# A 64-byte gap in on-chip memory ahead of the weight tiles of a streaming encoder

## The chip, the core and the metric

One core of a Trainium2 chip runs the kernel. The metric is the device time of one execution in microseconds (us). Five engines work side by side: TensorE (PE in the profile, with its weight loads listed apart as PEld), VectorE (DVE), ScalarE (ACT), GpSimd (POOL) and SyncE (SP, which only issues DMAs). All operands of the engines lie in SBUF, 128 partitions side by side, and a tile is a byte range that is the same in every partition.

## The reference

Two layers over 512 tokens of width 1024, in float32:

```
for l in (0, 1):
    h = rmsnorm(x, norm_mix_g[l])
    if l == 0:  mix = mlstm(conv+silu(h @ a_w_in)) * sigmoid(o)     # 4 heads of 192
    else:       mix = band_attention(h @ b_w_in, K, V, rel_bias)    # 12 heads of 64
    x = x + concat(mix, memory_attention(h, mem @ mem_w_kv[l])) @ w_out
    u, g = split(rmsnorm(x, norm_ffn_g[l]) @ ffn_w_up[l])           # 2 x 2816 columns
    x = x + (silu(causal_dwconv(g)) * u) @ ffn_w_down[l]
    if l == 0:  K, V = split(rmsnorm(x, kv_norm_g) @ w_kv)
return rmsnorm(x, final_g)
```

## The kernel before

Activations are kept transposed: a tile of 128 features by 512 tokens, `KT = 8` such tiles for the width. Each float32 operand of a product is split in two rounded halves, `hi` and `lo`, and each product is three matmuls, `hi*hi + lo*hi + hi*lo`. The rounding to `hi` is a copy on ScalarE (line 130), and `lo` is a subtraction on VectorE (line 131). The three matmuls are lines 169, 170 and 171:

```
def split(hi, lo, src, on_act=True, pinned=False):
    high = A.copy(hi, src) if on_act else V.tensor_copy(hi, src)
    low = V.tensor_tensor(out=lo, in0=src, in1=f(hi), op=ALU.subtract)
...
def mm3(o, lh, ll, rh, rl, first, last, more=False):
    nc.tensor.matmul(o, lh, rh, start=first, stop=False, skip_group_check=more)
    nc.tensor.matmul(o, lh, rl, start=False, stop=False, skip_group_check=more)
    nc.tensor.matmul(o, ll, rh, start=False, stop=last, skip_group_check=more)
```

A weight block of 128 by 1024 comes by a DMA of SP's queue into a raw tile `wr` (`load`, line 143) and is split by `parts` into `wh` and `wl`. In `project` and its relatives the blocks of `wh` and `wl` are the stationary operand, 128 columns at a time, and the activations (`u` tiles) stream past, 512 or 256 columns each. In `value_columns`, in the value products of the memory and in the last projection it is the other way round: `u` is stationary and `wh`, `wl` stream.

All tiles of one tag come from one pool with a fixed count of buffers:

```
bufs = {"wr": 3, "wh": 3, "wl": 3, "u": 57, "t": 8, "pt": 2, "s": 16, "rb": 3, "bias": 4}
```

`u` holds activations and their halves, `t` scratch, `pt` probabilities (and, in the channel mixer, raw gate weights), `s` small columns of 32 numbers (sums, reciprocals), `rb` the row of the norm, broadcast over the partitions, `bias` the exponents and relative biases that POOL's queue brings (lines 1029, 1325, 1407). Constants lie in a pool of their own ahead of these: `ident`, `ones`, `onesr` (a 128x128 tile of ones, the stationary operand where a sum over partitions is spread, lines 244 and 274), the columns of norm gains.

The pool lays its tags out in the order in which the program first asks for them, each with its count of buffers, so where a tile lies follows from the text. The built program has these offsets, in bytes in each partition (before the change):

| tag | bytes of one | first one at | modulo 512 |
|---|---|---|---|
| `ident`, `ones`, `onesr` | 512 | 16512, 17024, 17536 | 128 |
| `u` | 2048 | 20544 | 64 |
| `pt` | 10240 | 137280 | 64 |
| `wr` | 4096 | 157760 | 64 |
| `t` | 2048 | 170048 | 64 |
| `s` | 128 | 186432 | 64 |
| `wh` | 4096 | 188480 | 64 |
| `wl` | 4096 | 200768 | 64 |
| `rb` | 2048 | 213056 | 64 |
| `bias` | 2048 | 219200 | 64 |

The order of the work on PE, ACT and DVE is written out by hand in most of the kernel: generators for the attention heads are woven with generators for projections, and the channel mixer's steps are listed one by one. SP's loads run ahead as far as the three `wr` buffers let them.

Of the kernel before, what the change touches and what calls it, by code (L numbers as in the profile page):

```python
# [9 lines left out]
F32 = mybir.dt.float32  # L10
# [6 lines left out]
P = 128  # L17
# [38 lines left out]
def trunk(  # L56
# [22 lines left out]
    pool = ctx.enter_context(tc.tile_pool(name="pool", bufs=1))  # L79
    psum = ctx.enter_context(tc.tile_pool(name="psum", bufs=1, space=bass.MemoryType.PSUM))  # L80

    bufs = {"wr": 3, "wh": 3, "wl": 3, "u": 57, "t": 8, "pt": 2, "s": 16, "rb": 3, "bias": 4}
# [4 lines left out]
    def sb(tag, shape, dtype=F32):  # L87
        count[0] += 1
        return pool.tile(shape, dtype, tag=tag, name=f"{tag}{count[0]}", bufs=bufs[tag])
# [5 lines left out]
    def small(n=4):  # L95
        return sb("s", [P, 32])[:, :n]
# [278 lines left out]

    memT, xT = [], []
    norm = Norm()
    ss = small(2 * TT).rearrange("p (c t) -> p c t", c=2)

    def square(T, c, on_act):  # L380
# [1142 lines left out]
```

## Time and profile before

| | us |
|---|---|
| median of 3 runs | 1195.89 |
| lowest, highest | 1195.11, 1197.09 |
| the profiled execution: time | 1195.72 |
| its span, first to last instruction | 1194.0 |
| PE busy | 1183.5 (99%) |
| DVE busy | 961.7 (81%) |
| ACT busy | 725.2 (61%) |
| POOL busy | 130.3 (11%) |
| mean granted TensorE clock | 0.999 |

The profiled execution spends 1195.72 - 1194.0 = 1.72 us outside its span. A matmul is listed with the time from its start to the modelled end of its pipeline, so neighbours overlap, and PE's pace is read from the distance between starts. Under a line number stand all instructions that this line issued; names are the program's tiles without their buffer numbers, output first.

### The profile page before, as it was taken

The numbers are of one execution on the slowest core, as the hardware profiler recorded it, in microseconds if no ns is written. First come the engines' busy times: TensorE is split into PE (matmuls) and PEld (weight loads), VectorE is DVE, ScalarE is ACT, GpSimd is POOL, SyncE is SP. The second block draws the span as 40 slices with busy tenths as digits, with TensorE's granted clock in tenths as the row PEclk, the third lists the DMA queues.
The fourth block names the chain that finished last, engine by engine and source line by source line (L and its number), as shares of the span: only waits on it lengthen the run. The fifth ranks groups of instructions, "written<-read, shape, count | busy, mean of one in ns | idle before, by whom it ended". The sixth has DMA issues, their size and how long they took to land.

```text
span 1194.0 us, 18184 instructions
## 1 busy us (share of the span) xinstructions
PE 1183.5 (99%) x6719; PEld 1037.0 (87%) x6719; DVE 961.7 (81%) x1760; ACT 725.2 (61%) x1294; POOL 130.3 (11%) x222
## 2 busy tenths in 40 slices
PE   9999999999999999999999999999999999999997
PEld 9988888888899998999888888888889988999986
DVE  6877788788978888888698888997896888888855
ACT  5648677655656555555576677776565655555545
POOL 1211201010021111111020000101001011011100
PEclk9999999999999999999999999999999999999999
DMA  8645313444265676665464313246336455665551
GB/s 289 212 108 140 84 54 80 152 144 141 88 156 147 156 165 165 154 144 123 142 204 123 89 54 101 69 135 185 111 99 141 116 139 135 142 141 139 119 158 71
DMA packets 200155, 158.61 MB, mean 133 GB/s; under 512 B 8344, under 2 KB 179838, under 8 KB 200066
## 3 DMA queue, kind: packets, MB, share of 16 engines
q1 hardware_dynamic: 183906, 119.74, 34.1%
q0 software_dynamic: 15584, 36.67, 14.9%
q8 instruction: 53, 0.87, 0.3%
q10 hardware_dynamic: 576, 1.05, 0.2%
q14 instruction: 36, 0.29, 0.1%
HBM read 128.89 MB, written 32.46 MB: 135 GB/s over the span
## 4 chain that ended last, share of the span: by engine, by line
PE 92%; ACT 3%; DVE 2%; DMA 1%; SPq 1%; issue 0%; POOL 0%; POOLq 0%; DVEq 0%; ACTq 0%
PE pmm L169 15%; PE pmm L170 15%; PE pmm L171 15%; PE ptr L171 6%; PE ptr L169 6%; PE ptr L170 6%; PE pmm L785 6%; PE psc L171 5%; PE psc L170 5%; PE psc L169 5%; PE pmm L784 3%; PE psc L519 2%; PE ptr L1350 1%; DMA wr<-in_mem_w_kv_dram 1%; PE ptr L1371 1%; PE ptr L1372 1%
## 5 line engine op out<-in xcount | busy, mean ns | idle before, releaser
L169 PE MATMUL pmm<-u,wh 128*128 128x512 f32 (+1 forms) x872 | 309.1, 355 | 0.3 <-ACT u L130 0.2
L170 PE MATMUL pmm<-u,wh 128*128 128x512 f32 (+1 forms) x872 | 306.2, 351 | 0.0
L171 PE MATMUL pmm<-u,wl 128*128 128x512 f32 (+1 forms) x872 | 306.0, 351 | 0.0
L131 DVE TENSOR_TENSOR wl<-wr,wh 128x1024 fp32r<-128x1024 f32 (+3 forms) x172 | 199.8, 1163 | 57.0 <-ACT wh L130 55.0
L130 ACT CAST wh<-wr 128x1024 fp32r<-128x1024 f32 (+3 forms) x172 | 172.4, 1004 | 97.7 <-PE pmm L170 44.5
L171 PEld LDWEIGHTS pmm<-u,wl 128*128 128x128 f32 x872 | 164.5, 189 | 21.1
L169 PEld LDWEIGHTS pmm<-u,wh 128*128 128x128 f32 x872 | 164.5, 189 | 18.5 <-ACT u L130 1.1
L170 PEld LDWEIGHTS pmm<-u,wh 128*128 128x128 f32 x872 | 164.7, 189 | 18.2 <-DVE u L131 0.5
L169 PE MATMUL ptr<-u,wh 128*128 128x512 f32 x272 | 106.7, 392 | 0.0
L171 PE MATMUL ptr<-u,wl 128*128 128x512 f32 x272 | 106.1, 390 | 0.0
L753 POOL DMA_DIRECT2D xspill<-t x64 | 55.6, 869 | 461.1 <-ACT t L752 450.4
L170 PE MATMUL ptr<-u,wh 128*128 128x512 f32 x272 | 105.9, 389 | 0.0
L130 ACT CAST u<-pt 128x512 fp32r<-128x512 f32 x102 | 63.0, 620 | 46.8 <-DVE pt L875 46.7
L131 DVE TENSOR_TENSOR u<-pt,u 128x512 fp32r<-128x512 f32 x102 | 69.9, 688 | 11.2 <-ACT u L130 8.5
L169 PE MATMUL psc<-u,wh 128*128 128x256 f32 (+1 forms) x232 | 76.1, 328 | 0.0
L171 PE MATMUL psc<-u,wl 128*128 128x256 f32 (+1 forms) x232 | 75.9, 327 | 0.0
L170 PE MATMUL psc<-u,wh 128*128 128x256 f32 (+1 forms) x232 | 75.9, 327 | 0.0
L937 ACT ACTIVATE t<-t 128x512 f32<-128x512 f32 x34 | 21.6, 634 | 79.3 <-DVE t L660 79.3
L785 PE MATMUL pmm<-u,u 128*128 128x512 f32 x192 | 69.6, 397 | 0.0
L821 DVE TENSOR_TENSOR t<-t,pmm 128x256 f32<-128x256 f32 x72 | 30.2, 419 | 44.9 <-ACT t L819 44.8
L752 ACT COPY t<-ptr 128x512 f32<-128x512 f32 x64 | 37.4, 585 | 43.1 <-PE ptr L171 43.1
L660 DVE SCALAR_TENSOR_TENSOR t<-t,cols,t 128x511 f32<-128x511 f32 x80 | 59.7, 746 | 3.7 <-ACT t L667 3.7
(300 smaller groups left out, 2673.8 us busy)
## 6 DMA issues: line engine op xcount, KB each, us to landing
wr<-in_ffn_w_up_dram SPq DMA_DIRECT2D x54, 512.0 KB, 4.2
wr<-in_ffn_w_down_dram SPq DMA_DIRECT2D x38, 512.0 KB, 4.1
pt<-in_ffn_w_up_dram SPq DMA_DIRECT2D x34, 512.0 KB, 6.2
xspill<-t POOLq DMA_DIRECT2D x64, 256.0 KB, 5.2
wr<-in_a_w_in_dram SPq DMA_DIRECT2D x20, 512.0 KB, 3.7
xspill<-u POOLq DMA_DIRECT2D x32, 256.0 KB, 2.6
u<-xspill SPq DMA_DIRECT2D x32, 256.0 KB, 5.0
wr<-in_w_kv_dram SPq DMA_DIRECT2D x12, 512.0 KB, 3.7
```

Of the source, the lines that this page charges most:

```text
L130: high = A.copy(hi, src) if on_act else V.tensor_copy(hi, src)
L131: low = V.tensor_tensor(out=lo, in0=src, in1=f(hi), op=ALU.subtract)
L169: nc.tensor.matmul(o, lh, rh, start=first, stop=False, skip_group_check=more)
L170: nc.tensor.matmul(o, lh, rl, start=False, stop=False, skip_group_check=more)
L171: nc.tensor.matmul(o, ll, rh, start=False, stop=last, skip_group_check=more)
L519: nc.tensor.matmul(o, a, b, start=first and i == 0, stop=i == 1)
L660: V.scalar_tensor_tensor(acc[:, n:], src[:, : S - n], self.fw[:, c * FT + j : c * FT + j + 1], acc[:, n:], op0=ALU.mult, op1=ALU.add,)
L752: A.copy(t, o)
L753: G.dma_start(xspill[j], t, accum_op=ALU.add)
L784: nc.tensor.matmul(r[:, :H], w[1][:, k], p[i - 1][:, :H], start=False, stop=False, skip_group_check=True)
L785: nc.tensor.matmul(r, w[0][:, k], p[i - 1], start=False, stop=k == n - 1, skip_group_check=True)
L821: V.tensor_tensor(out=o, in0=o, in1=r[:, H:], op=ALU.add)
```

## The change

A tile of 16 numbers (64 bytes in each partition) is requested from the pool with a tag of its own, after `u`, `pt`, `wr` and `t` have been asked for, and ahead of the first `s`. Nothing writes or reads it.

```diff
     memT, xT = [], []
     norm = Norm()
+    pool.tile([P, 16], F32, tag="gap", name="gap", bufs=1)
     ss = small(2 * TT).rearrange("p (c t) -> p c t", c=2)
```

In the built program `s`, `wh`, `wl`, `rb` and `bias` start 64 bytes later than before (at 128 modulo 512); `u`, `pt`, `wr`, `t` and all constants lie where they lay. Every engine has the same instructions, in the same order and with the same waits; of the operands only these offsets differ. The line numbers after line 377 are higher by one.

## The prediction

> **What bounds the kernel now.** I read the page's busy shares first, then the chain of work that ended last, then what PE waited for.
>
> ```profile
> PE 1183.5 (99%) x6719; PEld 1037.0 (87%) x6719; DVE 961.7 (81%) x1760; ACT 725.2 (61%) x1294; POOL 130.3 (11%) x222
> PE 92%; ACT 3%; DVE 2%; DMA 1%; SPq 1%; issue 0%; POOL 0%; POOLq 0%; DVEq 0%; ACTq 0%
> 300.00:590.00 290.00, 290.00 (x1811) 262.16 (x1810) 239.02 (x381) 166.53 (x287) 42.13 (x56) 1.00 0.58 141
> 860.00:1160.00 300.00, 300.00 (x1855) 270.44 (x1854) 244.83 (x388) 170.63 (x293) 27.35 (x32) 1.00 0.54 132
> 1160.00:1194.00 34.00, 26.92 (x149) 22.44 (x148) 16.41 (x44) 17.01 (x37) 0.00 (x0) 0.95 0.16 62
> ```
>
> PE is busy for 1183.5 of 1194.0 us and carries 92% of the chain. The last three lines are from the busy time by stage (columns: length, then PE, PEld, DVE, ACT, POOL with counts, the granted clock, the DMA share, GB/s): in the two channel mixers PE has no gap at all, while DVE works 239.0 of 290 us and ACT 166.5. Of PE's 10.5 us of idle time 34.00 - 26.92 = 7.1 lie in the last 34 us. So the time is PE's pace, matmul after matmul. As no engine gets another instruction or another wait, only one question is left: does any instruction or transfer take another time when some of its operands lie 64 bytes further on?
>
> **How many instructions meet a moved tile.** The groups of weight loads give the count for `wh` and `wl`.
>
> ```profile
> L169 PEld LDWEIGHTS pmm<-u,wh 128*128 128x128 f32 x872 | 164.5, 189 | 18.5 <-ACT u L130 1.1
> L169 PEld LDWEIGHTS ptr<-u,wh 128*128 128x128 f32 x272 | 51.2, 188 | 8.5
> L169 PEld LDWEIGHTS psc<-u,wh 128*128 128x128 f32 x232 | 44.0, 190 | 4.5
> L784 PEld LDWEIGHTS pmm<-u,wl 128*128 128x128 f32 x96 | 18.3, 191 | 0.0
> L785 PEld LDWEIGHTS pmm<-u,wh 128*128 128x128 f32 x96 | 18.1, 189 | 3.4
> ```
>
> Lines 170 and 171 have as many as line 169, so 3 x (872 + 272 + 232) + 96 + 96 = 4320 of 6719 matmuls take their stationary operand from a moved tile. That makes the resolution of the question plain: 0.2% of the time, 2.4 us, about what a measurement of this kernel can tell from no change, is 2.4 / 4320 = 0.56 ns for each of these loads.
>
> **PE's pace before.** Two steady trains, in order of start (start us, duration us); the lines between go on in the same step.
>
> ```profile
> 601.16 0.39 PE L169 MATMUL pmm<-u,wh 128*128 128x512 f32 x1
> ...
> 605.92 0.39 PE L169 MATMUL pmm<-u,wh 128*128 128x512 f32 x1
> ...
> 394.28 0.28 PE L170 MATMUL pmm<-u,wh 128*128 128x256 f32 x1
> ...
> 395.48 0.28 PE L171 MATMUL pmm<-u,wl 128*128 128x256 f32 x1
> ```
>
> From 601.16 to 605.92 there are 21 starts, 4.76 / 21 = 0.2267 us each, for 512 columns; from 394.28 to 395.48 there are 10, 0.120 us each, for 256. The difference, 107 ns, is the price of 256 columns, so each matmul carries 120 - 107 = 13 ns that are not columns. In the first train ACT and DVE split the next block into `wh` and `wl` and DMAs fill `wr` at the same time, and the step stays the same: nothing that runs beside it is seen in it.
>
> **Stationary operands, 4320 loads.** The trace has no load from `wh` at the new place, but it has loads from a tile that lies as `wh` will: the constant `onesr`, at 128 modulo 512, with the streaming tiles at 64 modulo 512, which is just the relation after the change.
>
> ```profile
> L244 PEld LDWEIGHTS psc<-t,onesr x10: 186/188/192, 30.0 to 248.6; 128*128 128x128 f32 x10
> L274 PEld LDWEIGHTS psc<-t,onesr x6: 186/188/188, 280.2 to 841.6; 128*128 128x128 f32 x6
> 600.03 0.39 PE L170 MATMUL pmm<-u,wh 128*128 128x512 f32 x1
> 600.03 0.19 PEld L171 LDWEIGHTS pmm<-u,wl 128*128 128x128 f32 x1
> 280.21 0.39 PE L171 MATMUL pmm<-u,wl 128*128 128x512 f32 x1
> 280.43 0.63 PE L274 MATMUL psc<-t,onesr 128*128 128x512 f32 x2
> 626.09 0.39 PE L171 MATMUL pmm<-u,wl 128*128 128x512 f32 x1
> 626.32 0.65 PE L274 MATMUL psc<-t,onesr 128*128 128x512 f32 x2
> 248.11 0.39 PE L169 MATMUL ptr<-u,wh 128*128 128x512 f32 x1
> 248.33 0.40 PE L244 MATMUL psc<-t,onesr 128*128 128x512 f32 x1
> 248.57 0.39 PE L170 MATMUL ptr<-u,wh 128*128 128x512 f32 x1
> 248.80 0.39 PE L244 MATMUL psc<-t,onesr 128*128 128x512 f32 x1
> 157.63 0.39 PE L171 MATMUL pmm<-u,wl 128*128 128x512 f32 x1
> 157.86 0.40 PE L244 MATMUL psc<-t,onesr 128*128 128x512 f32 x1
> 133.86 0.39 PE L171 MATMUL pmm<-u,wl 128*128 128x512 f32 x1
> 134.09 0.40 PE L244 MATMUL psc<-t,onesr 128*128 128x512 f32 x1
> ```
>
> The load by itself takes 186 to 192 ns (min/median/max) from `onesr`, and 188 to 191 ns in the mean of the groups from `wh` and `wl` above. A load starts with the matmul ahead of it (600.03 and 600.03) and runs beside its stream, so what a bad place would cost shows in the distance from that matmul to the next. With `onesr` loading beside a `u` stream these distances are 280.43 - 280.21 = 0.22, 0.23, 0.22, 0.23, 0.23 and 0.23 us, mean 0.2267, against 0.2267 in the train. Starts are shown to 0.01 us, so one distance has a rounding error of some 0.004 us (standard deviation) and the mean of six 0.0016. I take 0 for each load, by these rows, and keep both ends: 1.6 ns less and 1.6 ns more, which is 7 us either way over 4320 loads. Neither is excluded: the fixed 13 ns leave room below.
>
> **The same tiles on ACT and DVE.** ACT will write and DVE read and write the moved `wh` and `wl`, and DVE, ACT the moved `s`, `rb`, `bias`.
>
> ```profile
> L131 DVE TENSOR_TENSOR wl<-wr,wh 128x1024 fp32r<-128x1024 f32 x143 | 174.9, 1223 | 49.2 <-ACT wh L130 47.3
> L130 ACT CAST wh<-wr 128x1024 fp32r<-128x1024 f32 x143 | 150.3, 1053 | 78.8 <-PE pmm L170 37.9 <-PE psc L171 16.5 <-issue 9.1
> L130 ACT CAST wh<-pt 128x1024 fp32r<-128x1024 f32 x34 | 36.0, 1058 | 0.0
> L231 DVE TENSOR_TENSOR t<-ident,s x10: 684/685/687, 28.0 to 247.7; 128x512 fp32r<-128x512 f32 x10
> L940 DVE TENSOR_TENSOR t<-t,t x34: 680/685/693, 359.7 to 1153.5; 128x512 f32<-128x512 f32 x34
> ```
>
> `ident` lies at 128 modulo 512, and a subtraction-like operation on it takes the 685 ns (median) of one whose operands all lie at 64. So DVE gets 0. No row has ACT at the new offset; its nearest bound is the 5 ns by which its two groups of casts differ, 177 x 5 = 0.9 us up or down, and it is hidden: ACT has 290 - 166.5 = 123 us of free time in the first mixer alone. If that cover failed, ACT's cast feeds DVE's subtraction and that PE, with 5 ns per block of 8 or more loads. I take 0.
>
> **Transfers into `bias`.** 16 + 12 + 2 transfers of POOL's queue end in a moved tile; those into `wr`, `u`, `pt`, `t` do not move.
>
> ```profile
> bias<-rep POOLq DMA_DIRECT2D x12, 256.0 KB, 3.3
> bias<-exponents POOLq DMA_DIRECT2D x4, 256.0 KB, 3.7
> L1029 POOL DMA_DIRECT2D bias<-exponents x16: 547/566/572, 83.0 to 193.7; - x16
>   POOL bias L1029: 93.6, 8
>   POOL t L1157: 35.9, 3
> ```
>
> The last two lines are all that waited for work on `bias`: POOL, for its buffers. No PE, ACT or DVE instruction is listed as waiting for one of these transfers to land. Bounds: below, nothing (no later start gets earlier); above, the 0.4 us between the two rows for each of 30, 12 us, all of it under a lead of up to four buffers. I take 0.
>
> The Trainium skill has a rule that speaks against the change here: "DMA: Bandwidth & Descriptors", section "How a descriptor splits into AXI transactions", says that a descriptor which doesn't start on a 256-byte boundary begins at the boundary below it, and that the bytes ahead still cost beats of 32 bytes. By that page a 2048-byte row goes from 64 + 2 beats to 64 + 4 beats, an estimate of 3% on such a transfer, and the sum would still be 0, as nothing waits for it; no run here shows transfers at two offsets.
>
> **The sum.** 0 + 0 + 0 on the profiled 1195.72 us. That execution is 0.17 us below the median of the runs, 1195.89, so the prediction is the median, 1195.9.
>
> **Rivals.** *Slower: a load from the new place drags PE.* Place: every load from `wh` and `wl`. For it speaks one distance: two `onesr` loads in succession, 280.43 with x2 taking 0.63 in all for matmuls of 0.39, so the second starts 0.24 us after the first instead of 0.227. If that is the offset, the price is 13 ns x 4320 = 56 us, 1252; if a tenth of it, 5.6 us, 1201.5. Against it stand the six distances of 0.22 to 0.23 ahead of `onesr` in the same relation of places. It decides from 0.56 ns for each load. *Faster: the 13 ns are a meeting of load and stream.* Before, the load and the stream beside it run over the same offsets modulo 512 from the same moment on; shifted, they would meet less. All of the 13 ns gone would be -56 us, 1140; a tenth -5.6 us, 1190.3. Against it: the same six distances keep the 13 ns. It decides from the same 0.56 ns. The Trainium skill, "SBUF — State Buffer", section "Who interferes with whom", says that PE and ACT wait for nobody and that only the port pair of VectorE and GpSimd is contended; by that rule neither rival exists, and the trace agrees as far as the steady 0.2267 us go. *The change does not do what it says*, the unused tile being dropped: the offsets in the built program speak against it, and it would give 1195.9 too, so it has no share of its own.
>
> **How the numbers follow.** No change over 0.2% (1193.5 to 1198.3): 0.62. It isn't more, since 0.56 ns decides and my rows resolve 1 to 2 ns. Slower: 0.21, of which somewhat over half lies within 7 us. Faster: 0.17, of which something under half lies within 6 us. The slower side has the larger share because it has a distance (0.24) for it, and the faster one none. The range from 1190.0 to 1203.0 takes in 0.62 + 0.11 + 0.07 = 0.80; its ends are about the 7 us of the bounds on the loads, the lower one cut by 1 us since the shorter step has no row for it.
>
> **What would show it.** Right: in the profile after, the steady trains of lines 169 to 171 keep 0.2267 and 0.120 us from start to start, the loads of `wh` and `wl` 188 to 191 ns, the split 1053 and 1223 ns, and PE's idle time 10 to 11 us. Wrong: another step in these trains, of even one nanosecond, with the loads' durations or without; or a wait of PE for line 130 or 131 that grew in the mixers, which would put it down to ACT or DVE; or a wait of ACT or DVE for a transfer into `bias`.

## The result: 0.6% slower, and the profile after

The changed kernel takes 1202.39 us (median of 4 runs, 1201.99 to 1204.43) against 1196.09 before (4 runs); the ratio is 1.0058, 95% interval 1.0046 to 1.0071. The forecast was no change at 1195.9. The time is inside the range given (1190 to 1203), but the direction is that of the rival on the slower side. The profiled execution took 1202.36 us with a span of 1200.6, at a mean granted clock of 0.999 as before.

The first lines of the page after, and the two channel mixers in the busy time by stage (length, then PE, PEld, DVE, ACT, POOL, each with its count of instructions):

```profile
PE 1190.9 (99%) x6719; PEld 1030.9 (86%) x6719; DVE 962.2 (80%) x1760; ACT 722.5 (60%) x1294; POOL 130.1 (11%) x222
PE 97%; ACT 1%; DVE 1%; DMA 1%; issue 0%; SPq 0%; POOL 0%; POOLq 0%; DVEq 0%; ACTq 0%
300.00:590.00 290.00, 290.00 (x1802) 258.64 (x1800) 240.98 (x384) 166.63 (x288) 42.03 (x56) 1.00 0.58 141
860.00:1160.00 300.00, 300.00 (x1856) 267.30 (x1855) 248.66 (x395) 172.56 (x296) 27.28 (x32) 1.00 0.55 130
```

PE is busy 7.4 us longer (1190.9 - 1183.5) with the same 6719 matmuls; its idle time went down, from 10.5 to 1200.6 - 1190.9 = 9.7 us. DVE and POOL have the same busy time within 0.5 us, ACT 2.7 us less. So nothing waits for anything new: PE itself got slower. The groups of instructions say where not to look:

```profile
L169 PEld LDWEIGHTS pmm<-u,wh 128*128 128x128 f32 x872 | 164.4, 189 | 20.8 <-ACT u L130 1.0
L131 DVE TENSOR_TENSOR wl<-wr,wh 128x1024 fp32r<-128x1024 f32 x143 | 174.6, 1222 | 51.1 <-ACT wh L130 49.5
L130 ACT CAST wh<-wr 128x1024 fp32r<-128x1024 f32 x143 | 149.5, 1047 | 88.4 <-PE pmm L170 41.9 <-PE psc L171 17.0 <-issue 11.0
```

A load from `wh` is listed with 189 ns as before, the subtraction with 1222 ns (1223), the cast with 1047 (1053). The loss is in the distance from one start to the next, called a *step* below; a *train* is an unbroken row of like matmuls. In PE's instructions in order of time (start us, duration us):

```profile
605.16 0.39 PE L171 MATMUL pmm<-u,wl 128*128 128x512 f32 x1
...
610.06 0.39 PE L171 MATMUL pmm<-u,wl 128*128 128x512 f32 x1
...
412.96 0.28 PE L171 MATMUL pmm<-u,wl 128*128 128x256 f32 x1
...
415.34 0.28 PE L171 MATMUL pmm<-u,wl 128*128 128x256 f32 x1
```

From 605.16 to 610.06 there are 21 starts, 0.2333 us each, where the prediction showed 0.2267: 512-column trains step 6.7 ns longer. From 412.96 to 415.34 there are 21 starts of 256 columns, 0.1133 us each, where it showed 0.120: 6.7 ns *shorter*. These two trains went opposite ways by the same amount.

Summed over all steps whose stationary operand is in `wh` or `wl` (starts in the trace are kept to the nanosecond; 74 of the 4320 steps, those with a stall in them, are left out): 2758 steps of 512 columns go from 631.4 to 644.6 us, mean 228.9 to 233.7 ns; 1488 steps of 256 columns from 178.1 to 171.9 us, mean 119.7 to 115.5 ns. That is +13.2 - 6.2 = +7.0 us, against 6.6 us between the spans. Over the same steps before and after, those with `u` on both sides hold theirs (184.2 and 184.4 us). Steps with `wh` or `wl` streaming and `u` stationary gain 0.3 us in all (70.6 and 70.9 us), again with two signs: 0.5 us more at 512 columns, 0.3 us less at 256. The means differ from the steady 0.2267 and 0.1133 because a train takes some steps to settle (in the trace of before the first step of a 512-column train takes 233.1 ns in the mean, the fourth 229.4, and those from the tenth on 226.7), and because not all 256-column trains after the change settle at 0.1133: many stay at 0.1178.

### The profile page after: what moved, and what is told of

Same layout as the page of the kernel before. It is cut to its first block, busy times and chain, and to the rows that moved or that the text cites. A ratio compares the mean times of both kernels' runs of the same rounds, so it can differ in the third digit from the quotient of the medians.

```text
span 1200.6 us, 18184 instructions
## 1 busy us (share of the span) xinstructions
PE 1190.9 (99%) x6719; PEld 1030.9 (86%) x6719; DVE 962.2 (80%) x1760; ACT 722.5 (60%) x1294; POOL 130.1 (11%) x222
## 4 chain that ended last, share of the span: by engine, by line
PE 97%; ACT 1%; DVE 1%; DMA 1%; issue 0%; SPq 0%; POOL 0%; DVEq 0%; POOLq 0%; ACTq 0%
PE pmm L169 16%; PE pmm L171 16%; PE pmm L170 16%; PE ptr L170 6%; PE ptr L171 6%; PE ptr L169 6%; PE pmm L786 6%; PE psc L169 5%; PE psc L171 5%; PE psc L170 5%; PE pmm L785 3%; PE psc L520 2%; PE ptr L1351 1%; PE ptr L1372 1%; PE ptr L1373 1%; PE ptr L603 1%
## 5 line engine op out<-in xcount | busy, mean ns | idle before, releaser
L169 PE MATMUL ptr<-u,wh 128*128 128x512 f32 x272 | 107.7, 396 | 0.0
L170 PE MATMUL ptr<-u,wh 128*128 128x512 f32 x272 | 107.5, 395 | 0.0
```

## The experiments

Below, *distance* is the byte address of the stationary operand less that of the streaming one, modulo 256. Before it is 0 everywhere in these products, after the change 64 where `wh` and `wl` are stationary (and 192 where they stream). The results of the products (`pmm`, `ptr`, `psc`) are tiles of a pool in PSUM, a memory apart from SBUF, which no edit touches. Where steps are given, they are means over steps chosen as above, for `wh` and `wl` stationary. Each ratio is to runs of the kernel before that were taken beside it, with medians from 1195.26 to 1196.09 us.

### Only the weight tiles

```diff
     ss = small(2 * TT).rearrange("p (c t) -> p c t", c=2)
+    pool.tile([P, 16], F32, tag="gap", name="gap", bufs=1)
 ...
         vws1 = [parts(vraw1[0])]
+        pool.tile([P, 112], F32, tag="gap2", name="gap2", bufs=1)
```

> Only wh and wl start 64 bytes later; a second gap of 448 bytes ahead of rb puts rb and bias back to where they were modulo 512, and s does not move. If PE's pace is set by the place of its weight tiles (by distance to the streaming tiles or by their own place): the same as the changed kernel, 512-column trains at 233 ns from start to start, 256-column trains at 113 to 118, ratio 1.005 to 1.007. If s, rb or bias (the small columns, norm rows, biases) carry the loss: trains back at 226.7 and 120 ns and ratio 1.000.

Measured: 1201.89 us, ratio 1.0054 (1.0039 to 1.0069); steps 233.7 and 115.5 ns, as in the changed kernel. The whole effect comes with `wh` and `wl`. The small columns, the norm rows and the biases have no part in it, and neither have the transfers into `bias`.

### Everything moved by the same 64 bytes

```diff
+    pool.tile([P, 16], F32, tag="gap", name="gap", bufs=1)
     memr, kraw = [], []
```

> The gap stands ahead of the first tile of the pool, so that u, pt, wr and t move by the same 64 bytes as s, wh, wl, rb and bias. If the distance between the weight tile and the streaming tile counts: distance 0 modulo 512 as before, trains at 226.7 ns and 120 ns, ratio 1.000 (within 0.002). If the place of the weight tile itself counts (128 modulo 512 instead of 64): as the changed kernel, 233 ns and 1.006.

Measured: 1194.71 us, ratio 0.9998 (0.9988 to 1.0007); steps 228.9 and 119.7 ns, as before. The weight tiles lie where the change puts them and nothing is lost: their own place does not count, only a distance to something that moved along.

### Which distance: the streaming tiles moved, the raw weights not

```diff
+    pool.tile([P, 48], F32, tag="gap", name="gap", bufs=1)
     memr, kraw = [], []
 ...
     vraw = [two_rows(mem_w_kv[0], MEM, u) for u in range(4)]
+    pool.tile([P, 16], F32, tag="gap2", name="gap2", bufs=1)
     kraw1 = [load(rows(mem_w_kv[1], 0, MEM, 4 * u, 4 * u + 4), 4, MEM) for u in range(2)]
```

> The streaming tiles u and pt move by 192 bytes and everything else, wr, t, s, wh, wl, rb and bias, stays where it was modulo 256 (a second gap of 64 bytes ahead of wr). So wh and wl are 64 bytes ahead of u, as after the change, but lie as before to wr and t, with which ACT and DVE work. If the distance between the stationary and the streaming operand of PE counts: 233 and 113 to 118 ns, ratio 1.005 to 1.006. If the distance between wr and wh, wl counts (ACT's and DVE's reads and writes): 226.7 and 120 ns, ratio 1.000.

Measured: 1201.99 us, ratio 1.0052 (1.0035 to 1.0068); steps 233.7 and 115.5 ns. With `wr`, `wh`, `wl` and `t` where they were to each other and only `u` and `pt` moved, the loss is the same. It is the distance between the two operands of a matmul, not that between the tiles with which ACT and DVE work.

### Other distances

```diff
-    pool.tile([P, 16], F32, tag="gap", name="gap", bufs=1)
+    pool.tile([P, 8], F32, tag="gap", name="gap", bufs=1)
```

This is the gap of 32 bytes, set against the changed kernel; those of 128, 192 and 256 bytes have 32, 48 and 64 numbers in place of 8.

> The gap is 32 bytes, half of the change. If SBUF is met in steps of 64 bytes or more, 32 bytes stay in the same step for half of the time or for all of it: paces of 226.7 and 120 ns or between these and 233.3 and 113, ratio 1.000 to 1.003. If the pace moves smoothly with the distance: halfway, 230 and 117 ns, ratio 1.003.

> The gap is 128 bytes: wh, wl, s, rb and bias are 128 bytes off the streaming tiles modulo 512. If only the distance modulo 128 counts: as before, 226.7 and 120 ns, ratio 1.000. If the pace moves on with the distance, another step of 16 PE clocks (6.7 ns) is to be seen in one of the trains: 512 columns at 220 or 240 ns, or 256 at 106.7 or 120, and the time leaves 1196 by 6 us or more. If any distance but 0 is bad: 233 ns and 1.006.

> The gap is 192 bytes: the weight tiles lie 192 bytes behind the streaming tiles, which modulo 256 is 64 bytes ahead of them. If the sign of the distance is of no account: as with 64 bytes, 512 columns at 233.3 ns, 256 columns at 113 to 118, ratio 1.005 to 1.006. If the time within 256 bytes counts, with its direction: another pair of paces, 220 ns for 512 columns being possible (16 PE clocks less than now), and then a ratio of 0.99 or less.

> The gap is 256 bytes. If the distance counts modulo 128 or 256: as before, 226.7 and 120 ns, ratio 1.000. If modulo 512 or more (the 128 columns of one load are 512 bytes in each partition): another pace than before, with the 512-column train anywhere from 220 to 240 ns.

Measured:

| gap, bytes | us | ratio (95%) | 512 columns, ns | 256 columns, ns |
|---|---|---|---|---|
| none | 1196.09 | | 228.9 | 119.7 |
| 32 | 1205.64 | 1.0088 (1.0074 to 1.0102) | 233.6 | 117.9 |
| 64 (the change) | 1202.39 | 1.0058 (1.0046 to 1.0071) | 233.7 | 115.5 |
| 128 | 1204.96 | 1.0078 (1.0063 to 1.0093) | 232.9 | 119.0 |
| 192 | 1195.80 | 1.0002 (0.9993 to 1.0012) | 230.8 | 116.2 |
| 256 | 1195.05 | 0.9997 (0.9987 to 1.0007) | 228.9 | 119.7 |

256 bytes are as good as none: of the distances tried, the pace repeats there and not at 128. Half of the change (32 bytes) costs more than the whole: the 512-column steps lose as much and the 256-column steps gain less. So it does not move smoothly, and the expected 1.000 to 1.003 were missed. At 192 the two kinds of step cancel, and a time of "no change" hides +5.1 us in the one and -5.2 us in the other (636.3 less 631.1 and 172.7 less 177.9 us, over the same steps); a time alone would have shown nothing there. 220 ns for 512 columns was not seen at any distance.

### One half alone

```diff
+    gaps = []
 ...
         hi = sb("wh", [P, D], F32R)[:, : a * b].rearrange("p (a b) -> p a b", a=a)
+        if not gaps:
+            gaps.append(pool.tile([P, 112], F32, tag="gap2", name="gap2", bufs=1))
 ...
     ss = small(2 * TT).rearrange("p (c t) -> p c t", c=2)
+    pool.tile([P, 16], F32, tag="gap", name="gap", bufs=1)
```

> Only wh starts 64 bytes later; wl, s, rb and bias stay at their places modulo 512. The three matmuls of a product use the halves hi, hi, lo (lines 169, 170, 171). If the distance between the next load and the stream beside it counts: in 512-column trains the steps 171 to 169 and 169 to 170 take 233 ns, 170 to 171 226.7, ratio near 1.004. If the distance between a matmul's own stationary operand and its stream counts: 169 to 170 and 170 to 171 take 233, 171 to 169 226.7, ratio near 1.004. If the train only knows one pace, set by the worst pair: all three at 233, ratio 1.006.

Measured: 1203.42 us, ratio 1.0069 (1.0055 to 1.0083). In this kernel the three matmuls are lines 173, 174, 175; a train of 512 columns in order of time:

```profile
310.23 0.39 PE L173 MATMUL psc<-u,wh 128*128 128x512 f32 x1
310.45 0.40 PE L174 MATMUL psc<-u,wh 128*128 128x512 f32 x1
310.69 0.40 PE L175 MATMUL psc<-u,wl 128*128 128x512 f32 x1
310.92 0.39 PE L173 MATMUL psc<-u,wh 128*128 128x512 f32 x1
```

One round takes 0.69 us, steps of 225, 236 and 232 ns to the nanosecond: a mean of 231.0, two thirds of the way from 226.7 to 233.3 as a charge on each load would have it. But the fast step is 173 to 174, which none of the three theories named: there both the matmul's own operand and the one being loaded are at 64. So a step cannot be told from the distance of one load. In other trains of the same kernel the mean is 233.3 ns (the last products of the first channel mixer, 601 to 626 us), and the 256-column steps are at 117.8 in the mean. The same distances have more than one steady pace. At one place the pace changes at a disturbance: the products from 258 to 282 us run at 233.3 ns, then come two loads of `onesr` (282.71 and 282.95), and from there to 340 us it is 231.1; two such loads at 846.8 us leave 233.3 as it was. The kernel with the gap of 192 bytes shows it twice: 228.9 ns up to two loads of `onesr` at 280.72 us and 233.3 from the next step on, and the same at 842.00, while two at 626.36 leave 228.9. So a short disturbance can move a train from one pace to another; what decides whether it does is not shown. Both kinds of step are worse than two thirds of the change would make them: the 512-column steps lose 10.6 us instead of 8.8 and the 256-column steps gain 2.9 instead of 4.2. That is why the ratio is above 1.004.

### The trains by themselves

```python
def train(name, n, distance):
    o = psum.tile([P, S], F32, tag="o", name=name, bufs=4)
    for i in range(N):                                   # N = 60
        at = i % 8 * P + distance(i) // 4
        k = i % 4 * S
        nc.tensor.matmul(o[:, :n], weight[:, at : at + P], stream[:, k : k + n], start=i == 0, stop=i == N - 1)
```

> No part of the reference is computed: after 20 warming matmuls there are 20 trains of 60 matmuls with nothing beside them, each with a load of 128 stationary columns, over a constant tile; ten trains of 512 and ten of 256 columns. The first eight of each have the stationary operand at 0, 32, 64 ... 224 bytes from the streaming one (modulo 256), the ninth only every twelfth at 64 and the others at 0, the tenth follows the pattern 64, 64, 0. If the pace is a matter of PE's own two reads: 226.7 and 120 ns at 0, 233 and 113 to 118 at 64, and the other distances as the gaps of 32, 128 and 192 bytes gave (512 columns 233, 233, 231 to 233; 256 columns 118, 119, 116). If ACT's and DVE's reads and writes beside the trains are needed for it: the same pace at all distances. Ninth train: if each load is charged for itself, 5 of 60 steps 6.7 ns longer; if a single odd load is free, as the loads of onesr were, 226.7 in the mean of all.

Measured: 227.78 us for the whole of it, one run. Some of the trains in order of time (start, length from the first start to the last end); `widea` is distance 0, `wideb` 32, `widec` 64, `wideg` 192, all of 512 columns; `halfa` is 0 and `halfc` 64 with 256 columns:

```profile
7.89 13.89 PE L97 MATMUL widea<-stream,weight 128*128 128x512 f32 x60
21.62 14.15 PE L97 MATMUL wideb<-stream,weight 128*128 128x512 f32 x60
35.61 14.16 PE L97 MATMUL widec<-stream,weight 128*128 128x512 f32 x60
49.61 14.20 PE L97 MATMUL wided<-stream,weight 128*128 128x512 f32 x60
...
91.59 13.91 PE L97 MATMUL wideg<-stream,weight 128*128 128x512 f32 x60
105.34 14.16 PE L97 MATMUL wideh<-stream,weight 128*128 128x512 f32 x60
119.33 13.85 PE L97 MATMUL widesingle<-stream,weight 128*128 128x512 f32 x60
133.02 14.03 PE L97 MATMUL widethirds<-stream,weight 128*128 128x512 f32 x60
146.89 7.35 PE L97 MATMUL halfa<-stream,weight 128*128 128x256 f32 x60
154.08 7.26 PE L97 MATMUL halfb<-stream,weight 128*128 128x256 f32 x60
161.18 7.23 PE L97 MATMUL halfc<-stream,weight 128*128 128x256 f32 x60
168.25 7.20 PE L97 MATMUL halfd<-stream,weight 128*128 128x256 f32 x60
```

From the start of `widec` to that of `wided` there are 60 steps in 14.00 us, 233.3 ns each. No other engine is busy beside these trains and the granted clock is 1.00 throughout, so the effect is PE's alone: it follows the distance between the operand that it loads and the one that it streams. Means of 40 steps late in each train, from the starts to the nanosecond:

| distance | 0 | 32 | 64 | 96 | 128 | 160 | 192 | 224 |
|---|---|---|---|---|---|---|---|---|
| 512 columns, ns | 226.7 | 233.3 | 233.3 | 234.3 | 232.4 | 233.3 | 228.8 | 233.3 |
| 256 columns, ns | 120.0 | 118.3 | 117.8 | 117.3 | 118.7 | 120.0 | 117.8 | 117.8 |

0 is the best of the eight for 512 columns and the worst, with 160, for 256. The loads themselves are listed with 187 to 193 ns in all of them. The ninth train (`widesingle`, one load in twelve at 64) is the key to the prediction's mistake: the step beside the odd load takes 225 ns, less than the usual 226.7, and the four after it 236, 229, 232 and 231 before the train is back at 226.7. The odd load costs 1153 - 5 x 226.7 = 20 ns, all of it in steps in which PE loads and streams at distance 0 again. So neither theory for this train holds: a load is not charged for itself (6.7 ns), and a single odd load is not free. With 256 columns the like train gains 6.5 ns for each odd load. The tenth train (`widethirds`, distances 64, 64, 0) steps 225, 236 and 232 ns, just as the kernel with one half moved does: that pattern too is PE's own.

### A faster version

```diff
-    def parts(raw, pinned=False):
+    def parts(raw, pinned=False, off=0):
         _, a, b = raw.shape
-        hi = sb("wh", [P, D], F32R)[:, : a * b].rearrange("p (a b) -> p a b", a=a)
-        lo = sb("wl", [P, D], F32R)[:, : a * b].rearrange("p (a b) -> p a b", a=a)
+        hi = sb("wh", [P, D + 64], F32R)[:, off : off + a * b].rearrange("p (a b) -> p a b", a=a)
+        lo = sb("wl", [P, D + 64], F32R)[:, off : off + a * b].rearrange("p (a b) -> p a b", a=a)
 ...
-            self.a11, self.a12 = zip(*(self.halves(t) for t in parts(self.up)))
+            self.a11, self.a12 = zip(*(self.halves(t) for t in parts(self.up, off=16)))
 ...
-            self.s1, self.s3 = zip(*(self.halves(t) for t in parts(self.s13)))
+            self.s1, self.s3 = zip(*(self.halves(t) for t in parts(self.s13, off=16)))
```

The blocks of the second layer's memory keys and values get `off=16` in the same way; those of the first layer lie in `u` tiles and stay.

> A version meant to be faster than both: wh and wl are 256 bytes longer, and blocks that meet 256-column streams (the keys and values of the memory, and in the channel mixer the blocks of the up weights and of their first sums) begin 64 bytes into them; blocks for 512-column streams and the value columns stay at distance 0. If each product's pace follows its own distance: 512 columns keep 226.7 ns, 256 columns go from 120 to 113 to 118, some 4 ns x 1450 = 6 us less, 1190, ratio 0.995. If the 113 to 118 ns need the slower 512-column trains around them: no gain, ratio 0.999 to 1.001.

Measured: 1190.36 us (5 runs, 1189.85 to 1192.34), ratio 0.9962 (0.9949 to 0.9974): faster than both kernels.

```profile
PE 1178.3 (99%) x6719; PEld 1031.6 (87%) x6719; DVE 961.6 (81%) x1760; ACT 723.2 (61%) x1294; POOL 130.0 (11%) x222
300.00:590.00 290.00, 290.00 (x1821) 261.70 (x1820) 240.51 (x384) 166.43 (x288) 42.02 (x56) 1.00 0.60 144
860.00:1160.00 300.00, 300.00 (x1866) 270.00 (x1865) 243.39 (x385) 169.52 (x290) 27.28 (x32) 1.00 0.55 132
```

PE works 5.2 us less than before (1178.3 against 1183.5), and in each mixer's stretch it gets through some ten matmuls more (1821 against 1811, 1866 against 1855). The 512-column steps stay at 228.9 ns in the mean and the 256-column ones go to 116.4: 173.2 us against 178.1, 4.9 us of the 6 that were expected. The steps of 113.3 ns that fill whole trains after the change are rarer here (the bare train at 64 has 117.8 too), so the first theory holds in kind, at four fifths of its size.

## Why the prediction was wrong

*What bounds the kernel* was right, and so was the point of decision, 0.56 ns for each load: the net was 7.0 us over the 4246 steps that are in the sums, 1.6 ns each. The sign that it named for being wrong, another step in the trains with the loads' durations kept, is what came.

*The step that failed is "Stationary operands, 4320 loads".* It took six isolated loads of `onesr`, at just the distance that the change makes, and read the distance from the start of the matmul ahead of each to its own start: 0.2267 us, nothing. The likeness of the places was right, and so were the numbers within the error that it gave (to the nanosecond the six are 226, 226, 226, 231, 226 and 230, in the mean 227.5). The place to read was not: as the ninth train shows, the price falls on the steps that follow, and what counts is the pace into which a whole train settles. The trace of before had it, in the lines after such loads. Here is a pair that the prediction didn't show:

```profile
841.37 0.39 PE L171 MATMUL pmm<-u,wl 128*128 128x512 f32 x1
841.60 0.63 PE L274 MATMUL psc<-t,onesr 128*128 128x512 f32 x2
842.06 0.39 PE L169 MATMUL pmm<-u,wh 128*128 128x512 f32 x1
...
843.68 0.39 PE L170 MATMUL psc<-u,wh 128*128 128x512 f32 x1
```

From 841.37 to 843.68 there are ten steps, 2.31 us; ten steps of 0.2267 would be 2.27. The two loads of `onesr` cost 40 ns here, and none of it in the one step that was measured. The pairs that the prediction showed cost 40 ns (280.43), 47 (626.32) and 13 (248.33 and 248.80, with one other load between), counted in the same way until the step is back at 226.7: more than nothing each time, but not one price.

In whole trains the term put at 0 measures +4.8 ns for each 512-column step (233.7 less 228.9) and -4.2 ns for each 256-column step.

*A second omission in the same step:* it weighed the six loads in 512-column trains only, and charged all 4320 alike. A third of the loads stand in 256-column trains, which go the other way. With the right sign for each the sum is +13.2 - 6.2; with one price for all, as in the rivals, neither the size nor the chance of a gain from the mixture could be seen.

*That the time lies inside the range is luck.* The range's ends rest on 1.6 ns either way for each load; +4.8 and -4.2 ns lie both outside that, and only because they cancel in part is the net 1.6 ns for each, 7.0 us. The slower rival's 1201.5 is close to 1202.39 for the same reason.

*The same tiles on ACT and DVE* and *the transfers into `bias`* were right at 0: 1222 ns and 1047 ns, and the time stayed when `rb` and `bias` were put back. The 256 KB transfers into `bias` land after 3.7 us (from `rep`) and 3.8 us (from `exponents`), where it was 3.3 and 3.7; in the run that puts `bias` back it is 3.2 and 4.2. A difference of 3%, which the prediction estimated for them, can't be told in this scatter. That estimate also applies the rule that the prediction quoted from the Trainium skill, "DMA: Bandwidth & Descriptors", section "How a descriptor splits into AXI transactions", to the end that is written, while the passage speaks of bytes that are fetched.

*The rivals.* The slower one had the place (every load from `wh` and `wl`) and the sign, and the 0.24 us after a first `onesr`, its only evidence, was a true sign and had been outvoted six to one by distances read at a place that could not show the price. Its prices, 13 ns or a tenth of it, were guesses; measured is half of 13 ns in steady 512-column trains. The faster one has the sign of the 256-column trains, where up to 6.7 of the 13 ns go; that load and stream meet less there, its reason, is not shown. The prediction quoted the Trainium skill, "SBUF — State Buffer", section "Who interferes with whom", which has it that PE waits for nobody and lists its two reads, of the streaming and of the loaded operand, as independent. Here page and measurement differ: in the bare trains PE's step goes from 226.7 to 233.3 ns by the distance of these two reads alone. The measurement decides.

*What stays open.* Why the two reads disturb each other, and why the pace repeats at 256 bytes and at no smaller distance that was tried, is not shown. Nor is it shown what picks one of several paces at the same distance (113.3 or 117.8 ns for 256 columns at 64; 228.8 or 233.3 for 512 columns at 192, both within one kernel).

## What to carry to other kernels

In this kernel, where PE has no gaps, the byte distance between its stationary and its streaming operand is a tuning knob worth about half a per cent: 0 modulo 256 for 512-column streams and 64 for 256-column streams, set by a few unused bytes in front of a tile. Try it for each kind of stream, and try it last, since an unrelated change of a tile's size ahead of the weights moves it too, unless it is a multiple of 256 bytes. And read a disturbance in a pipelined train over the steps that come after it, not at the one that looks odd.

## What the runs showed of the hardware that was not expected

- PE's step depends on the distance of its two operands: 226.7 to 234.3 ns for 512 columns and 117.3 to 120.0 ns for 256 (bare trains), with the load listed at 187 to 193 ns whatever the distance.
- 256 bytes of distance are as good as 0 (ratio 0.9997), 128 are not (1.0078), and 32 cost more than 64 (1.0088 and 1.0058).
- In a bare 512-column train at distance 0 a single load at distance 64 costs 20 ns, all of it in the four steps after the one beside the load. Pairs of such loads inside the kernel cost 13 to 47 ns together.
- A step does not follow from one load's distance: with distances 64, 64, 0 in turn the steps are 225, 236 and 232 ns, in the kernel and in a bare train.
- Two odd loads can leave a train at another pace for good: with the gap of 192 bytes it goes from 228.9 to 233.3 ns at two of three such pairs.
